# Reordering the recurrence stage of a hybrid encoder block: a planner that follows operands, scores ahead of a bank's first values, merged inverse products

## The chip, the core and the metric

The kernel runs on one core of a Trainium2 chip. The metric is device time in microseconds (us) of one execution. Before the change it is 1988.1 us, the median of three runs (1982.59 to 1990.96). A core has a matrix engine (TensorE, PE in the profile, with PEld its weight loads), a vector engine (DVE), a scalar engine (ACT), GpSimd (POOL), and SyncE (SP), which here issues the DMAs. Each works through its own instructions in order and waits on semaphores for the others. Matrix products land in PSUM, which has eight banks of 128x512 float32.

## The reference, cut to what matters

One encoder layer for a sequence of 1024 positions of width 1024, batch 1:

```
h  = RMSNorm(x);  P = h @ W_in            # latents, RWKV columns, two gates
A  = attention(P)                          # 8 heads, softmax over all 1024 keys
B  = WKV-7 scan forward + WKV-7 scan backward   # 8 heads of 64 x 64 state
     state = state * w_t + (state a_t) b_t^T + v_t k_t^T ;  out_t = state r_t
y  = (sig(gA) * (A @ W_o[:512]) + sig(gB) * (B @ W_o[512:])) @ W_merge
x  = x + y;  x = x + GatedMLP_dwconv3(RMSNorm(x))
```

All arithmetic is float32. The kernel splits large factors into a high and a low part and takes three products for one (the words "hi", "lo", `ph`, `pl`, `wlo` are such parts).

## The kernel before, in words

There are four stages in time. First come the projections and the preparation of all heads' operands. The second stage is the **recurrence stage** that the change is about: it runs on the trace from about 346 us to about 1160 us. Then come the mixture of the branches with `w_merge`, and the feed-forward network.

In the recurrence stage two kinds of work share PE. The **dense** work is a generator, `dense()`: the gate projections (`gates`, line 1153 on, by `mmk`, lines 278 to 281), then `attention` (line 1235 on), then the first branch's output products (`branch0`). The **recurrence** is done in chunks of 64 positions, eight units of 128 positions, both directions at once. For each unit a job `prep_a` makes what the chunks need: decays and keys (`a0` to `a3`), a masked product `NM` (`nm`, `nz`, line 858), which goes through DRAM so that 128 blocks of 16x16 lie one per partition, and the inverse of each block by 15 vector steps (`inv`, tiles `Ti`, `tm`). The inverses go through DRAM again (`dU`, `dT`; step `tq`) and come back as `Un` and `TT` (step `u`, lines 889 to 894: 14 DMAs). Then small products join the blocks to 64x64 inverses: step `p` (line 901), `x` (lines 907 and 914), `y` (lines 925 and 926, into one bank, two products per chunk and half), `t` (line 936). Jobs `prep_b` make the masked products of a chunk (`er`, `ak`, `bt`). The generator `chain` is the recurrence itself: eight hops per unit, each one bank of small products (lines 1019, 1028, 1032, 1046, 1055, 1066) and its eviction. `gnorm` normalizes a unit's output; the last unit's goes on to the mixture.

The order of PE, DVE, ACT and POOL in this stage is that of the program text as it is emitted; only SP's order is the compiler's. A **planner** (line 1423 on) chooses at each turn what to emit, by a clock `now` of its own in estimated ns. `now` moves on by the cost that each generator yields (213 for a product of 512 columns). The wrapper `Clocked` adds up an estimate for DVE, ACT and POOL (`V.t`, `S.t`, `G.t`): it starts an instruction at the later of the engine's last end and `now`. A step of `prep_a` or `prep_b` is due when the steps it needs are seen, when the delay that the step before yielded is over, and when its engine is at most `SLACK` ahead of `now`. A hop of the chain is due when the engines' estimated ends plus `HOP` are past and 1500 ns of dense work (`DENSE`) have gone by since the hop before. If nothing is due, `fill` emits the next piece of dense work. Where the dense work of the last 3400 ns is under 1300 ns, hops and the steps in `HEAVY` wait.

In `attention` a step is one score block (three products, lines 1289 to 1291, in one of three banks `st`), two exponentials or one and a copy, and the low part; four steps later its values are added into the bank `po` (three products, lines 1247 to 1249). After eight of them (one half of the queries of one head) the bank is evicted by a DVE copy `pv` and an ACT logarithm `rc`, and the next half's first values start it anew. There is one `po` bank. The next head's score maxima (`maxima`, line 1217: a product and a DVE reduction) are put beside the steps 3 to 13.

The tile pool `wk` holds one buffer per tag, so a new tile with a tag waits for the readers of the old one. Before, `Un` was one lasting tile of 128x16x32, zeroed once, and the sum `U` of step `x` took the tag `Ti` over from the inverse.

Of the kernel before, what the change touches and what calls it, by code (L numbers as in the profile page):

```python
# [23 lines left out]
NCH = 16  # L24
# [23 lines left out]
LAG = 4  # L48
AHEAD = 6
DENSE = (1500,) * 8  # L50
SLACK = 1500
# [3 lines left out]
CARRY = 3000  # L55
DELAY = {
# [29 lines left out]
def block_kernel(ctx: ExitStack, tc: tile.TileContext, a):  # L86
    nc = tc.nc
    now, ends = [0.0], [0.0]

    class Clocked:  # L90
# [5 lines left out]
        def __getattr__(self, name):  # L96
            f = getattr(self.eng, name)

            def call(*args, **kw):
                o = kw["in_"] if name == "tensor_reduce" else kw["out"] if "out" in kw else args[0] if args else None  # L100
                if hasattr(o, "shape"):
                    self.t = max(self.t, now[0]) + self.fixed + self.each * math.prod(o.shape[1:])
                    ends[0] = max(ends[0], self.t)
                return f(*args, **kw)  # L104
            return call

    V, S, G = Clocked(nc.vector, 140, 1.04), Clocked(nc.scalar, 140, 0.92), Clocked(nc.gpsimd, 100, 2.35)
# [101 lines left out]
    def mm3(ps, wh, wl, xs, first=True, last=True):  # L209
        n = len(xs)  # L210
        for k, (xh, xl) in enumerate(xs):
            ws = slice(k * 128, (k + 1) * 128)
            for hs in halves():
                nc.tensor.matmul(ps[:, hs], wh[:, ws], xh[:, hs], start=(first and k == 0), stop=False)
                nc.tensor.matmul(ps[:, hs], wh[:, ws], xl[:, hs], start=False, stop=False)
            for hs in halves():
                nc.tensor.matmul(ps[:, hs], wl[:, ws], xh[:, hs], start=False, stop=(last and k == n - 1))

    def mm32(ps, w, x, first=True, last=True):
        for hs in halves():  # L220
            nc.tensor.matmul(ps[:, hs], w, x[:, hs], start=first, stop=last)
# [53 lines left out]
    def mmk(outs, wh, wl, x, first, last):  # L275
        xh, xl = x
        for o, hs in zip(outs, HT):
            nc.tensor.matmul(o, wh, xh[:, hs], start=first, stop=False)  # L278
            nc.tensor.matmul(o, wh, xl[:, hs], start=False, stop=False)  # L279
        for o, hs in zip(outs, HT):  # L280
            nc.tensor.matmul(o, wl, xh[:, hs], start=False, stop=last)  # L281
# [5 lines left out]
    with pool("xp") as xp:  # L287
# [61 lines left out]
        for step in XORDER:  # L349
# [10 lines left out]
            else:  # L360
                for hs in HT:
                    ss = ss1()
                    nc.tensor.matmul(ss, onef, acc[:, hs], start=True, stop=True)
# [84 lines left out]
    def gsum(wts, parts):  # L448
        ss = ss1()
        for i, x in enumerate(parts):  # L450
            nc.tensor.matmul(ss, wts, x, start=(i == 0), stop=(i == 1))
# [4 lines left out]
    def mul(ps, w, x, **kw):  # L456
        now[0] += 213 if w.dtype == R else 853
        return nc.tensor.matmul(ps, w, x, **kw)
# [291 lines left out]
    Un = cbp.tile([128, NCH, 32], F32, name="Un")  # L750
    G.memset(Un, 0.0)
# [9 lines left out]
    now[0] = V.t = S.t = G.t = 0.0  # L761
    wpool["g"] = ctx.enter_context(pool("gp", side="right"))
# [43 lines left out]
    def prep_a(n, q):  # L806
# [4 lines left out]
        yield 0, 3000  # L811
# [41 lines left out]
        for c0_ in (0, 8):  # L853
            ps = scb()
            p3 = ps.rearrange("p (c t) -> p c t", t=C)
            for c in range(8):
                for h, hs in enumerate(H):
                    nc.tensor.matmul(p3[hs, c, :], BK[c0_ // 8][hs, c, H[h]], AXk[c0_ // 8][hs, c, :], start=True, stop=True)
# [29 lines left out]
        TT = TTt[n % 2]  # L888
        for g in range(8):
            rows, b = slice(16 * g, 16 * g + 16), g % 4  # L890
            if b != 3:
                nc.sync.dma_start(Un[rows, :, b % 2 * 16:b % 2 * 16 + 16], dU[g].rearrange("c t j -> t c j"))
            nc.sync.dma_start(TT[rows, :, b * 16:b * 16 + 16], dT[g].rearrange("c j t -> j c t"))
        yield 0, 4500
# [5 lines left out]
        for c, r, b in each4:  # L900
            nc.tensor.matmul(p3[r:r + 32, c], NM[r:r + 16, c, b:b + 32], Un[r:r + 16, c, 0:16], start=True, stop=True)
        S.activation(P, p3, AF.Copy, scale=cst[:, C_TI + 1:C_TI + 2])
        yield 1100, 300
        px = scb()[:, 0:256].rearrange("p (c j) -> p c j", j=16)
        for c, r, b in each4:
            if b == 0:
                nc.tensor.matmul(px[r:r + 32, c], TT[r:r + 32, c, 0:32], P[r:r + 32, c], start=True, stop=True)
        U = wk.tile([128, NCH, 16], F32, tag="Ti", name="U")
        for h in range(2):
            ia = slice(h * 64, h * 64 + 32)  # L910
            V.tensor_tensor(out=U[ia], in0=px[ia], in1=Un[ia, :, 0:16], op=add)
        py = scb()[:, 0:256].rearrange("p (c t) -> p c t", t=16)
        for c, r, b in each4:
            nc.tensor.matmul(py[r:r + 16, c], P[r:r + 32, c], TT[r:r + 32, c, b + 16:b + 32], start=True, stop=True)
# [7 lines left out]
        for c in range(NCH):  # L922
            for h in range(2):
                ia, ib = slice(h * 64, h * 64 + 32), slice(h * 64 + 32, h * 64 + 64)
                nc.tensor.matmul(p3[ib, c, 0:16], NM[ia, c, 32:64], U[ia, c], start=True, stop=True)
                nc.tensor.matmul(p3[ib, c, 16:32], NM[ia, c, 32:64], Un[ia, c, 16:32], start=True, stop=True)
# [6 lines left out]
        for c in range(NCH):  # L933
            for h in range(2):
                ia, ib = slice(h * 64, h * 64 + 32), slice(h * 64 + 32, h * 64 + 64)
                nc.tensor.matmul(p3[ia, c], Y[ib, c, :], TT[ib, c, 32:64], start=True, stop=True)
# [6 lines left out]
    def prep_b(n, q, hf):  # L943
# [27 lines left out]
        for c in range(8):  # L971
            for p3, hs in zip(two_, H):
                nc.tensor.matmul(p3[:, c], BK[hs, c, :], AXr[hs, c], start=True, stop=True)
# [8 lines left out]
        for c, d, i in each8:  # L982
            for h, hs in enumerate(H):
                nc.tensor.matmul(p3[H[1 - h], c, :], BK[hs, c, H[1 - h]], AXk[hs, c, :], start=True, stop=True)
# [6 lines left out]
        for d in range(2):  # L991
            ps = scb()
            p3 = ps.rearrange("p (c t) -> p c t", t=128)
            for i in range(4):
                nc.tensor.transpose(p3[:, i, :], BK[:, 4 * d + i, :], ident)
# [11 lines left out]
    def chain(n, q, osb):  # L1007
# [6 lines left out]
        def values(i, RR):  # L1014
            ps = v3(scb())
            vv = q[i][4]
            for s, d, c in EACH:
                for h in range(2):
                    nc.tensor.matmul(ps[H[1 - h], s, :], vv[:, d, c, :], ctr[:, H[h]], start=(s == 0), stop=(s == 7))
# [3 lines left out]
        def chunk_out(i, first, RR):  # L1023
            ct = ctb()
            AXr, Er = q[i][0:2]
            for s, d, c in EACH:
                for h, hs in enumerate(H):
                    nc.tensor.matmul(ct[hs, s, :], RR[h][:, s, 1, :], Er[:, d, c, h, :], start=(s == 0), stop=(first and s == 7))
            if not first:
                for s, d, c in EACH:  # L1030
                    for h, hs in enumerate(H):
                        nc.tensor.matmul(ct[hs, s, :], RR[h][hs, s, 0, :], AXr[hs, s, :], start=False, stop=(s == 7))
# [5 lines left out]
        for i in range(2):  # L1038
# [4 lines left out]
            for s, d, c in EACH:  # L1043
                for h, hs in enumerate(H):
                    ks = H[1 - h] if first else slice(0, 128)
                    nc.tensor.matmul(ct[hs, s, :], Ek[ks, d, c, h, :], RR[h][ks, s, 0, :], start=(s == 0), stop=(s == 7))
# [6 lines left out]
            for s, d, c in EACH:  # L1053
                for hs in H:
                    nc.tensor.matmul(ct[hs, s, :], TT[hs, 8 * i + s, :], rh[hs, s, :], start=(s == 0), stop=(s == 7))
# [8 lines left out]
            for s, d, c in EACH:  # L1064
                for h, hs in enumerate(H):
                    nc.tensor.matmul(ct[hs, s, :], BT[:, d, c, hs], RR[h][:, s, 1, :], start=(s == 0), stop=(s == 7))
# [20 lines left out]
    def gnorm(n, osb):  # L1087
        if n == NU // 2:
            xb.extend([[place(f"h{x}{4 + p}", f"ob{x}") for x in "hl"] for p in range(NPAIR - 1)])
        for d in range(2):  # L1090
# [10 lines left out]
            nc.tensor.matmul(ps, b64r.bitcast(F32), sq, start=True, stop=True)  # L1101
# [12 lines left out]
            for p in range(NPAIR):  # L1114
                cp_ = slice(128 * p, 128 * p + 128)
                nc.tensor.matmul(ps[:, cp_], g2[:, cp_], gl, start=True, stop=True)
# [93 lines left out]
    def maxima(h):  # L1210
# [3 lines left out]
        for qt in range(8):  # L1214
            for i2, hs in enumerate(halves()):
                ps = pt()
                nc.tensor.matmul(ps, qh[0:96, qt * 128:(qt + 1) * 128], kh[0:96, hs], start=True, stop=True)  # L1217
# [6 lines left out]
        nc.tensor.transpose(pm[0:8, 0:128], mx, ident)  # L1224
# [8 lines left out]
    o0, o3 = [], []  # L1233

    def attention():
# [3 lines left out]
        def values(h, q2, kt, ph, pl):  # L1239
# [7 lines left out]
            nc.tensor.matmul(po[0], vhk, ph, start=(kt == 0), stop=False)  # L1247
            nc.tensor.matmul(po[0], vhk, pl, start=False, stop=False)
            nc.tensor.matmul(po[0], vlk, ph, start=False, stop=(kt == 7))
            if kt == 7:  # L1250
# [4 lines left out]
                act(rc[own], po[0][oth], AF.Ln)  # L1255
                if i == 1:
# [16 lines left out]

        def low():
# [3 lines left out]
        for h in range(8):  # L1278
            qh, kh = qk[h % 2]
            nxt = maxima(h + 1) if h < 7 else iter(())  # L1280
            for q2 in range(2):
                qs = HT[q2]
                for kt in range(8):
                    if len(late) == LAG:
# [4 lines left out]
                    nc.tensor.matmul(ps, kh[:, ks], qh[:, qs], start=True, stop=False)  # L1289
                    nc.tensor.matmul(ps, kh[:, ks], ql[:, qs], start=False, stop=False)  # L1290
                    nc.tensor.matmul(ps, kl[:, ks], qh[:, qs], start=False, stop=True)
# [21 lines left out]
                    cost = 640  # L1313
                    late.append((h, q2, kt, ph, pl))
                    step = q2 * 8 + kt
# [4 lines left out]
                    for _ in range(2 if 3 <= step < 11 else 1 if step in (12, 13) else 0):  # L1320
                        cost += next(nxt, 0)
# [104 lines left out]
    B_STEPS = (("b0", 1, None), ("b1", 2, V), ("b2", 1, None), ("er", 1, V), ("ak", 1, V), ("bt", 2, S))  # L1426
# [717 lines left out]
```

## Time and profile before

| what | before |
|---|---|
| median of 3 runs | 1988.1 us |
| the profiled execution's own time | 1986.8 us |
| its span in the trace | 1985.0 us |
| PE busy, whole span | 1859.7 us (94%) |
| DVE, ACT, POOL busy | 1224.6, 870.5, 652.9 us (62%, 44%, 33%) |
| mean granted clock of PE | 0.964 |
| HBM read and written | 144.64 and 59.41 MB |

The profile is of one execution. A row of a group has the line, the engine, the operation, the tiles (out<-in), the shape and the count; then busy time of the group in us, mean ns of one instruction, and the idle time of its engine just ahead of these instructions with what ended it. Where the helper at line 104 records the instruction, all of DVE, ACT and POOL stand under L104 and are told apart by tiles. "issue" is a wait for nothing that the profile shows. A float32 product appears as two records. The granted clock is a share of full speed.

### The profile page before, as it was taken

To read this page: it belongs to the slowest core of one execution; us is meant where nothing else is said; L and a number is where in the kernel's file an instruction comes from. 1 tells how busy PE (TensorE), PEld (TensorE's weight loads), DVE (VectorE), ACT (ScalarE), POOL (GpSimd) and SP (SyncE) were. 2 spreads that over 40 slices of the span, in tenths; PEclk is the share of its full clock that TensorE was granted. 3 is DMA by queue.
4 is the path that set the end of the run, shared out by engine and by line. 5 is a ranking of instruction groups with operands and counts; after the bars stand their busy time and mean duration, and the time that the engine had idled before them with its cause. 6 is when DMAs were issued, how large, how long until landed. Compare 5 with 4: busy or idle time off the path is not lost. (4 is left out here: it accounts for less than half of the span.)

```text
span 1985.0 us, 37748 instructions
## 1 busy us (share of the span) xinstructions
PE 1859.7 (94%) x15440; PEld 1484.7 (75%) x15440; DVE 1224.6 (62%) x1837; ACT 870.5 (44%) x1378; POOL 652.9 (33%) x550
## 2 busy tenths in 40 slices
PE   7889999899999899989989999997999999999998
PEld 5656667677778677777777787775888888888886
DVE  7557666436436466767674345578667667666677
ACT  5576577123223156566666644543233233232331
POOL 7435554322221223343433332235422322322221
PEclk9889999889999898999899999999999999999999
DMA  4136544844454625353432675111111111111112
GB/s 154 36 120 198 176 157 157 227 113 113 121 141 105 176 42 130 80 144 84 112 92 80 215 247 195 41 66 37 49 64 48 48 61 51 48 59 53 48 54 101
DMA packets 260636, 210.71 MB, mean 106 GB/s; under 512 B 127144, under 2 KB 205032, under 8 KB 260464
## 3 DMA queue, kind: packets, MB, share of 16 engines
q1 hardware_dynamic: 260464, 208.31, 35.1%
q8 instruction: 121, 1.98, 0.4%
q14 instruction: 51, 0.42, 0.1%
HBM read 144.64 MB, written 59.41 MB: 103 GB/s over the span
## 5 line engine op out<-in xcount | busy, mean ns | idle before, releaser
L104 POOL TENSOR_TENSOR wlo<-wraw,whi 128x512 fp32r<-128x512 f32 x118 | 161.0, 1365 | 633.0 <-ACT whi L104 613.0
L278 PE MATMUL st<-hh,whi 128*128 128x512 f32 x408 | 175.7, 431 | 22.9 <-ACT hh L104 9.0
L279 PE MATMUL st<-hl,whi 128*128 128x512 f32 x408 | 165.6, 406 | 0.7 <-DVE hl L104 0.7
L104 DVE TENSOR_TENSOR x<-b,x 128x512 f32<-128x512 f32 x176 | 119.2, 686 | 54.6 <-PE b L1817 54.6
L104 POOL TENSOR_TENSOR pl<-pe,ph 128x512 fp32r<-128x512 f32 x64 | 84.3, 1316 | 207.5 <-ACT ph L104 188.8
L281 PE MATMUL st<-hh,wlo 128*128 128x512 f32 x408 | 141.7, 402 | 0.4 <-POOL wlo L104 0.4
L278 PEld LDWEIGHTS st<-hh,whi 128*128 128x128 f32 x408 | 80.1, 196 | 51.5 <-issue 10.8
L104 ACT CAST whi<-wraw 128x512 fp32r<-128x512 f32 x118 | 72.7, 618 | 104.6 <-PE po L279 29.0
L281 PEld LDWEIGHTS st<-hh,wlo 128*128 128x128 f32 x408 | 79.7, 196 | 19.5 <-POOL wlo L104 1.3
L279 PEld LDWEIGHTS st<-hl,whi 128*128 128x128 f32 x408 | 80.3, 197 | 17.6 <-DVE hl L104 1.7
L104 DVE TENSOR_REDUCE mx<-sc 128x1 f32<-128x512 f32 x128 | 81.7, 681 | 12.3 <-PE sc L1217 11.9
L104 POOL TENSOR_TENSOR wl<-wraw,wh 128x512 fp32r<-128x512 f32 x22 | 28.9, 1314 | 179.5 <-ACT wh L104 169.7
L1247 PE MATMUL po<-ph,vhh 128*128 128x512 f32 x128 | 58.9, 460 | 17.6 <-ACT rc L104 17.6
L104 DVE TENSOR_TENSOR u<-b,p 128x512 f32<-128x512 f32 x42 | 29.0, 691 | 72.0 <-PE b L1722 69.4
L1815 PE MATMUL b<-sh,wh 128*128 128x512 f32 x176 | 69.1, 392 | 4.2 <-ACT sh L104 4.2
L1816 PE MATMUL b<-sl,wh 128*128 128x512 f32 x176 | 69.3, 394 | 0.8 <-DVE sl L104 0.8
L1815 PE MATMUL b<-sh,whi 128*128 128x512 f32 x176 | 68.6, 390 | 1.3 <-DVE x L104 1.3
L1817 PE MATMUL b<-sh,wl 128*128 128x512 f32 x176 | 69.0, 392 | 0.0
L1816 PE MATMUL b<-sl,whi 128*128 128x512 f32 x176 | 68.5, 389 | 0.0
L1817 PE MATMUL b<-sh,wlo 128*128 128x512 f32 x176 | 68.5, 389 | 0.0
L104 ACT CAST whi<-s 128x512 fp32r<-128x512 f32 x33 | 20.5, 622 | 89.7 <-PE b L1816 44.0
L1289 PE MATMUL st<-qh,kh 128*128 128x512 f32 x128 | 59.2, 462 | 0.0
(496 smaller groups left out, 5415.4 us busy)
## 6 DMA issues: line engine op xcount, KB each, us to landing
wraw<-w_in SPq DMA_DIRECT2D x64, 256.0 KB
wraw<-w_fd SPq DMA_DIRECT2D x44, 256.0 KB
AA<-w_fu SPq DMA_DIRECT2D x41, 256.0 KB
A<-w_fg SPq DMA_DIRECT2D x41, 256.0 KB
ld<-d_x SPq DMA_DIRECT2D x32, 256.0 KB
d_gate<-gt SPq DMA_DIRECT2D x32, 256.0 KB
xt<-xT SPq DMA_DIRECT2D x8, 512.0 KB
d_s<-sg SPq DMA_DIRECT2D x8, 512.0 KB
```

Of the source, the lines that this page charges most:

```text
L104: return f(*args, **kw)
L278: nc.tensor.matmul(o, wh, xh[:, hs], start=first, stop=False)
L279: nc.tensor.matmul(o, wh, xl[:, hs], start=False, stop=False)
L281: nc.tensor.matmul(o, wl, xh[:, hs], start=False, stop=last)
L1247: nc.tensor.matmul(po[0], vhk, ph, start=(kt == 0), stop=False)
L1289: nc.tensor.matmul(ps, kh[:, ks], qh[:, qs], start=True, stop=False)
L1815: nc.tensor.matmul(b, wh[:, ws], xh[:, hs], start=(k == 0), stop=False)
L1816: nc.tensor.matmul(b, wh[:, ws], xl[:, hs], start=False, stop=False)
L1817: nc.tensor.matmul(b, wl[:, ws], xh[:, hs], start=False, stop=(k == 1))
```

## The change

The diff has these parts; a long run of lines only renames `nc.tensor.matmul` to `E.matmul`, where `E` is a wrapper that issues the same instruction.

- **Estimates that follow operands.** `Clocked` now starts an instruction no earlier than the estimated end of the writers of its operands, by a table `wrote` of tile names. `E` notes in `needs_pe` when the operands of a PE step are there, and `now` is raised to it before the step's cost is added.
- **Constants and rules of the planner.** `SLACK` goes from 1500 to 2500. A new rule (`BATCH`) holds the steps `er`, `ak`, `bt` and `gnorm` back once dense work has begun since the last step or hop, until 2500 of it have gone by. Step `a1` of the first unit is due 18000 after `a0`, not 3000.
- **Attention.** Where the next values are a bank's first (`kt` is 0), the scores and up to two maxima come ahead of them, and the planner may put hops and any steps in between while the estimate says that the bank is not yet evicted by more than 200 (`dense_at`). Maxima stand at steps 3 to 12, not 3 to 13, in the same number.
- **Inverse products.** Step `p` is due 6000 after step `u`, not 4500; step `x` 1500 after `p`, not 300. `Un` becomes a tile of tag `Ti`, zeroed on POOL for each unit; its DMAs are emitted ahead of those of `TT`. `U` and the other part of `Un` now lie side by side in a lasting tile `U2`, and step `y` is one product of 32 columns where two of 16 were.

```diff
-SLACK = 1500
+SLACK = 2500
+BATCH = 2500
...
-                    self.t = max(self.t, now[0]) + self.fixed + self.each * math.prod(o.shape[1:])
+                    out = kw["out"] if "out" in kw else args[0]
+                    names = [x.tensor.name for x in (*args, *kw.values()) if x is not out and hasattr(x, "tensor")]
+                    self.t = max(self.t, now[0], *(wrote.get(x, 0) for x in names)) + self.fixed + self.each * math.prod(o.shape[1:])
                     ends[0] = max(ends[0], self.t)
+                    wrote[out.tensor.name] = self.t
...
+            def call(out, a, b, **kw):
+                needs_pe[0] = max(needs_pe[0], wrote.get(a.tensor.name, 0), wrote.get(b.tensor.name, 0))
+                wrote[out.tensor.name] = 0
+                return f(out, a, b, **kw)
...
-        yield 0, 3000
+        yield 0, 3000 if n else 18000
...
+        Un = wk.tile([128, NCH, 16], F32, tag="Ti", name="Un")
+        G.memset(Un, 0.0)
+        for g in (0, 2, 4, 6, 1, 5):
+            dst = U2[:, :, 16:32] if g % 2 else Un
+            nc.sync.dma_start(dst[16 * g:16 * g + 16], dU[g].rearrange("c t j -> t c j"))
         for g in range(8):
-            rows, b = slice(16 * g, 16 * g + 16), g % 4
-            if b != 3:
-                nc.sync.dma_start(Un[rows, :, b % 2 * 16:b % 2 * 16 + 16], dU[g].rearrange("c t j -> t c j"))
-            nc.sync.dma_start(TT[rows, :, b * 16:b * 16 + 16], dT[g].rearrange("c j t -> j c t"))
-        yield 0, 4500
+            nc.sync.dma_start(TT[16 * g:16 * g + 16, :, g % 4 * 16:g % 4 * 16 + 16], dT[g].rearrange("c j t -> j c t"))
+        yield 0, 6000
...
-        yield 1100, 300
+        yield 1100, 1500
...
-            V.tensor_tensor(out=U[ia], in0=px[ia], in1=Un[ia, :, 0:16], op=add)
+            V.tensor_tensor(out=U2[ia, :, 0:16], in0=px[ia], in1=Un[ia], op=add)
...
-                nc.tensor.matmul(p3[ib, c, 0:16], NM[ia, c, 32:64], U[ia, c], start=True, stop=True)
-                nc.tensor.matmul(p3[ib, c, 16:32], NM[ia, c, 32:64], Un[ia, c, 16:32], start=True, stop=True)
+                E.matmul(p3[ib, c], NM[ia, c, 32:64], U2[ia, c], start=True, stop=True)
...
+        def after():
+            if late and len(late) == LAG:
+                h, q2, kt, ph, pl = late[0]
+                dense_at[0] = max(wrote.get(ph.tensor.name, 0), wrote.get(pl.tensor.name, 0), 0 if kt else po.get("t", 0))
...
-                    if len(late) == LAG:
+                    step = q2 * 8 + kt
+                    if len(late) == LAG and late[0][2]:
                         values(*late.pop(0))
                         yield 640
...
+                    cost = 640
+                    for _ in range(2 if 3 <= step < 11 else 1 if step in (11, 12) else 0):
+                        cost += next(nxt, 0)
+                    if len(late) == LAG:
+                        after()
+                        yield cost
+                        values(*late.pop(0))
+                        cost = 640
...
-                    for _ in range(2 if 3 <= step < 11 else 1 if step in (12, 13) else 0):
-                        cost += next(nxt, 0)
+                    if len(late) == LAG and late[0][2]:
+                        after()
                     yield cost
...
-            now[0] += x[0]
+            now[0] = max(now[0], needs_pe[0]) + x[0]
...
-            if light and (j is norm or j.steps[j.k][0] in HEAVY):
+            if light and (j is norm or j.steps[j.k][0] in HEAVY) or apart and (j is norm or j.steps[j.k][0] in LATER):
                 continue
...
-                if t <= now[0] and due <= 0 and not thin:
+                blocked = dense_at[0] > now[0] + 200
+                if t <= now[0] and (blocked or due <= 0 and not thin):
                     break
-                x = prepare(thin or sparse and t < math.inf)
+                x = prepare(not blocked and (thin or sparse and t < math.inf), not blocked and 0 < alone[0] < BATCH and due > -math.inf)
```

More of the change, by code (lines that the diff above doesn't have):

```diff
@@ L87, in block_kernel @@
     nc = tc.nc
-    now, ends = [0.0], [0.0]
+    now, ends, needs_pe, wrote = [0.0], [0.0], [0.0], {}
     class Clocked:
@@ L277, in mmk @@
         for o, hs in zip(outs, HT):
[L278 to L279 removed]
+            E.matmul(o, wh, xh[:, hs], start=first, stop=False)
+            E.matmul(o, wh, xl[:, hs], start=False, stop=False)
         for o, hs in zip(outs, HT):
[L281 removed]
+            E.matmul(o, wl, xh[:, hs], start=False, stop=last)
     cqps = [big(), big()]
@@ L1027, in chunk_out @@
                 for h, hs in enumerate(H):
-                    nc.tensor.matmul(ct[hs, s, :], RR[h][:, s, 1, :], Er[:, d, c, h, :], start=(s == 0), stop=(first and s == 7))
+                    E.matmul(ct[hs, s, :], RR[h][:, s, 1, :], Er[:, d, c, h, :], start=(s == 0), stop=(first and s == 7))
             if not first:
@@ L1233, in block_kernel @@
     o0, o3 = [], []
+    dense_at = [0.0]
     def attention():
@@ L1488, in run @@
         def run(self):
-            ends[0] = now[0]
+            ends[0], needs_pe[0] = now[0], 0
             x = next(self.gen, None)
@@ L1512, in block_kernel @@
     recent = []
+    alone = [0.0]
     def fill():
         nonlocal due
+        needs_pe[0] = dense_at[0] = 0
         x = next(dn, None)
@@ L1520, in fill @@
         else:
-            now[0] += x * 1.065
+            now[0] = max(now[0], needs_pe[0]) + x * 1.065
             due -= x
+            alone[0] += x
             recent.append((now[0], x))
@@ L1547, in block_kernel @@
                     sparse += 1
+                    alone[0] = 0.0
             if k == 4 and u:
@@ L1551, in block_kernel @@
                 osb = wk.tile([128, 2, 512], F32, tag="osb", name="osb")
-            ends[0] = now[0]
+            ends[0], needs_pe[0] = now[0], 0
             x = next(ch, None)
@@ L1556, in block_kernel @@
             hops = 8 * u + min(k + 1, 7)
-            now[0] += x
+            now[0] = max(now[0], needs_pe[0]) + x
+            alone[0] = 0.0
             ready = max(now[0], ends[0] + x) + HOP
@@ L1721, in quarter @@
             for m, (wt, x) in enumerate(((w[0], xh), (w[0], xl), (w[1], xh))):
-                nc.tensor.matmul(b, wt[:, ws], x, start=(first and k == 0 and m == 0), stop=(k == 3 and m == 2), skip_group_check=True)
+                E.matmul(b, wt[:, ws], x, start=(first and k == 0 and m == 0), stop=(k == 3 and m == 2), skip_group_check=True)
     ps7 = big4()
```

91 lines of the change are left out of this document (49 added, 42 removed).

## The prediction

> **What bounds the kernel now.** I read the page first, then the table of stretches, then PE's waits inside the recurrence stage. The page gives the span, PE at 94%, and PE's own instruction loads (its 30880 records make 1.98 MB, so 64 bytes each).
>
> ```profile
> span 1985.0 us, 37748 instructions
> PE 1859.7 (94%) x15440; PEld 1484.7 (75%) x15440; DVE 1224.6 (62%) x1837; ACT 870.5 (44%) x1378; POOL 652.9 (33%) x550
> ...
> q8 instruction: 121, 1.98, 0.4%
> ```
>
> The stretches (columns: PE, PEld, DVE, ACT, POOL busy, granted clock, DMA share, GB/s) show the stage that changes, and the one after it:
>
> ```profile
> 346.00:1130.00 784.00, 722.37 (x10654) 581.19 (x10652) 434.94 (x860) 350.92 (x628) 235.75 (x253) 0.94 0.47 122
> 1130.00:1200.00 70.00, 70.00 (x315) 57.68 (x314) 35.11 (x45) 33.45 (x45) 23.95 (x23) 1.00 0.74 248
> ```
>
> PE is the bound here: no other engine is busy for much over half. So only three things can be won: PE's idle time (784.0 - 722.4 = 61.6 us), the part of the clock that is not granted (784 x 0.06 = 47 us if PE has work), and PE work that is dropped. The waits of PE in this stage, longest first, say where the idle time is (us in total, times, longest):
>
> ```profile
> PE po L1247 <- ACT rc L104: 17.6, 10, 4.3
> PE sc L914 <- issue: 11.2, 4, 3.8
> PE st L278 <- ACT whi L104: 8.8, 2, 8.6
> PE sc L901 <- DMA Un<-dU: 8.2, 7, 1.9
> PE ct L1046 <- DVE mx L104: 4.9, 3, 2.9
> PE sc L926 <- issue: 3.0, 1, 3.0
> PE sc L907 <- issue: 2.2, 3, 1.0
> ```
>
> These seven rows are 55.9 of the 61.6 us, and every row but the fifth is at a place that the change touches: the first values of a bank, the inverse products, the start of the first unit. The clock goes with them:
>
> ```profile
> 358.80:369.00 10.20, 5.19 (x12) 4.14 (x13) 5.49 (x8) 3.25 (x6) 5.16 (x6) 0.50 0.88 255
> 724.00:727.40 3.40, 1.43 (x6) 0.67 (x4) 2.53 (x5) 1.95 (x4) 0.00 (x0) 1.00 0.11 39
> 727.40:734.20 6.80, 6.80 (x62) 5.76 (x63) 1.36 (x3) 2.14 (x5) 1.27 (x1) 0.50 0.18 41
> 734.20:737.60 3.40, 3.40 (x45) 2.55 (x44) 2.89 (x4) 1.32 (x3) 1.06 (x2) 1.00 0.00 0
> ```
>
> After a stretch of 3.4 us in which PE worked for 1.43 us the clock is at 0.50 for 6.8 us, though PE is busy throughout them, and then full again. A stall of 2 us is thus paid a second time.
>
> **The change part by part.** All is reckoned against the profiled execution (1986.8 us, span 1985.0), which is 1.3 us under the median of the three runs (1988.1); that difference I leave out.
>
> *Merged products.* Step `y` now has two products of 16 columns per chunk and half, and will have one of 32, the shape that step `t` has on the same 32x32 tiles:
>
> ```profile
> L925 PE MATMUL sc<-U,NM 32*32 32x16 f32 x512 | 17.3, 179 | 0.0
> L936 PE MATMUL sc<-TT,Y 32*32 32x32 f32 x512 | 10.0, 195 | 0.0
> ```
>
> The two old products alternate, so the busy time of the one row covers both. The new step costs what `t` costs: 17.3 - 10.0 = 7.3 us saved, all on PE. It also drops 1024 of PE's records (512 products, 512 weight loads), 64 KB of instructions.
>
> *The first unit's `a1` at 18000.* Today DVE reaches the scan of the first unit before its DMA has landed, and ACT and the next weights' high part queue behind it:
>
> ```profile
> 359.73 2.34 DVE L104 TENSOR_TENSOR_SCAN ld<-smask,ld 128x512 f32<-128x512 f32 x2 [8.94 <-DMA ld<-d_s]
> 361.03 0.63 ACT L104 ACTIVATE Pp<-ld 128x512 f32<-128x512 f32 x1 [9.01 <-DVE ld L104]
> 363.81 0.80 PE L278 MATMUL st<-hh,whi 128*128 128x512 f32 x1 [8.56 <-ACT whi L104]
> ```
>
> With 15 us more of dense work ahead of it, the scan stands behind the landing at 359.7 (the stage begins near 346, so its place is near 364). PE's 8.6 us go, and with them the stretch at half clock, 10.2 us, worth 5.1. Ends: 0 (another load is then late) and -13.7; I take -11, near the full price, because the cover of 4 us is real but not large.
>
> *Scores and maxima ahead of a bank's first values.* The bank's eviction waits in DVE's queue:
>
> ```profile
> 724.26 0.39 PE L1291 MATMUL st<-qh,kl 128*128 128x512 f32 x1
> 724.66 0.67 DVE L104 COPY RR<-ct 64x512 f32<-64x512 f32 x1
> 725.26 0.67 DVE L104 COPY pv<-po 64x512 f32<-64x512 f32 x1
> 725.97 0.59 ACT L104 ACTIVATE rc<-po 64x512 f32<-64x512 f32 x1
> 726.62 0.50 PE L1247 MATMUL po<-ph,vhh 128*128 128x512 f32 x1 [1.97 <-ACT rc L104]
> L1217 PE MATMUL sc<-kh,qh 96*128 96x512 f32 x128 | 41.0, 402 | 1.1 <-DMA qh<-d_qrh 1.1
> ```
>
> One more score block (three products that follow each other at about 0.23 us, 0.7 us) and one maximum (41.0/128 = 0.3 us) now stand between: 1.0 us against a mean stall of 1.76, so at most 10 us of 17.6 without more. The planner may add a hop or a preparation step there, so I take -12; ends 0 and -17.6. The held-back exponential of that score block is not needed until four steps later, which hides it.
>
> *Later inverse products, `Un` first.* SP issues the 14 DMAs of step `u` one after another:
>
> ```profile
> L892 SPq DMA_DIRECT2D Un<-dU x48: 302/447/1346, 405.2 to 1068.6; - x48
> L104 POOL MEMSET Un<- x1: 527/527/527, 345.9 to 345.9; 128x512 f32 x1
> ```
>
> The last part that `p` reads was issued twelfth and is now fourth: 8 x 0.447 = 3.6 us earlier, and `p` is 1.5 us later. The longest wait is 1.9, so of 8.2 us I take -7 (if the compiler keeps SP's old order, the 1.5 us alone leave a little). `TT` lands up to 2.2 us later (its first part goes from second to seventh place), but it is read in `x`, which is put off by 1.5 and 1.2 us. The wait that comes in: POOL zeroes `Un` (half of 527 ns, eight times, 2 us) once `Ti` has gone to DRAM; behind it on POOL stand the low parts of weights and exponentials, and PE waits for those. POOL is 33% busy, and step `u` comes 2500 after `tq`; I price it at 0, and at 2 us a unit, 16 us, if that cover is gone.
>
> *The waits on nothing, "issue" (16.4 us).* In the longest of them an instruction load lands (the DMA view of 501.9 to 505.7), in the middle of a run of small products:
>
> ```profile
> 500.76 1.14 PE L914 MATMUL sc<-TT,P 32*16 32x16 f32 x96
> 505.69 0.40 PE L914 MATMUL sc<-TT,P 32*16 32x16 f32 x28 [3.79 <-issue]
> q8 instruction: 1, 0.02, 1.5%
> ```
>
> One load is 1.98 MB/121 = 16 KB, 256 records. By the code steps `p` and `x` have 64 and 96 products, at four records each (two products, two weight loads) 256 and 384 records within a few us, beside a DMA queue full of other things. With 1.2 us more of dense work (few records) between `p` and `x`, and step `y` halved, some of it goes: ends 0 and -16.4, I take -6. The Trainium skill (Runtime: NRT & Kernel Launch, Instruction fetch mechanics) says that crossing a block of instructions costs one DMA tail-bump, "mostly hidden". By it this term would be 0 and the sum 6 us higher; the trace, with 3.79 us of PE idle around such a load, does not agree.
>
> *The clock.* Of the 47 us, 5.1 are counted above; 42 are left. The waits of the last three terms fall by 25 of 42.2 us. A stretch of half clock can outlive a shortened stall, so I take a third of the 42, -14; ends +5 and -42.
>
> *The planner.* Following operands, `SLACK`, `BATCH` and `dense_at` add no instruction. They let DVE run 1000 ns deeper behind PE, and small products share four banks with the maxima: the fifth row of the waits (4.9 us, 3 times, 1.6 each) is such a wait. I reckon six more of them, +10; ends 0 and +25.
>
> Sum: -7.3 - 11 - 12 - 7 - 6 - 14 + 10 = -47.3, so 1986.8 - 47.3 = 1939.5, rounded 1940 us.
>
> **The rivals.**
>
> *The chain falls behind the dense work* (slower). The end of the stage needs both:
>
> ```profile
> L104 POOL TENSOR_TENSOR osb<-gbo,osb x8: 456/462/477, 862.1 to 1152.0; 128x128 fp32r<-128x128 f32 x8
> L281 PE MATMUL po<-o,wlo x16: 388/389/398, 1107.8 to 1158.8; 128*128 128x512 f32 x16
> 613.40:661.60 48.20, 9.02 (x30) 1.00 0.42 119
> ```
>
> The last unit's output is done at 1152.5, the last dense product starts at 1158.8: a margin of 6.3 us. In the order the chain moves back by 15 us at the first unit and by 1.5 + 1.2 = 2.7 us for each of eight units, 36.6 in all. And the inverse of a unit lasts 48.2 us for 9.0 us of DVE (the third row, its `tm` instructions alone): the planner decides its pace. Later estimates of DVE hold it back, the larger `SLACK` lets it go; if the first wins by 5.5 us a unit, 44 more, the lag is 80.6 and the time 1940 + 80.6 - 6.3 = 2014 us. It decides slower from a lag of 6.3 + 47 = 53 us on. For it: the margin is small. Against it: 39 us of each inverse are waiting that the larger `SLACK` can shorten.
>
> *The waits change place* (about the same). The idle times of bank, `Un` and issue come back at other products, the clock stays, and the +10 is paid: 1986.8 - 7.3 - 11 + 10 = 1978.5 us. For it: DVE and ACT still do the same work, and the eviction above waited behind a hop's copy, not behind PE.
>
> *The clock stays as it is*: 1940 + 14 = 1954 us. The half stretches would then come from the small products themselves. The Trainium skill (TensorE: Matmul & The Clock Gate, HAM oscillation — how this bites in real kernels) gives the rule as no idle gaps of PE over about 3.4 us; by it only the longest stalls would count. The row at 724 has a stall of 1.97 us and then 0.50, which speaks against it, so it has a small chance.
>
> *The clock comes back whole*: 1940 - 28 = 1912 us. For it: the stretches of 0.50 above each follow a stall that the change aims at. Against it: the small products stay.
>
> **How the numbers follow.** A measurement of this kernel tells about 0.5% (10 us) from no change, so the bounds are 1978 and 1998 us. Chances: the forecast 0.46, the clock stays 0.12, the clock comes whole 0.10, the waits change place 0.16 (0.04 of it faster, 0.12 the same), the chain behind 0.16 (a lag under 45 us is still faster, 0.02; up to 63 the same, 0.02; beyond it slower, 0.12). Faster: 0.46 + 0.12 + 0.10 + 0.04 + 0.02 = 0.74; the same 0.12 + 0.02 = 0.14; slower 0.12. The range goes from 1912 (half of the whole-clock case below it, 0.05) to 1996 (0.12 above it): 0.17 left out.
>
> **What would show it.** Right: step `y` at about 10 us in all, in half the records; no idle of 8 us near 355; the wait of the values on `rc` under 6 us; the wait for `Un` near 1; mean clock of the stage 0.95 to 0.97; PE's idle time in the stage near 35 us. Wrong: a wait of PE on `mx` or on the low parts above 15 us, stretches of 0.50 as many as before, or PE idle at the end of the stage with `gnorm` as releaser. If the first values still wait 15 us, the eviction is late through DVE's queue, and not for want of PE work.

## The result, and the profile after

The kernel after takes 1939.12 us (median of four runs, 1933.54 to 1941.06); the kernel before, with one more run on the same chip, 1986.78 us. The ratio is 0.9756, with a 95% interval of 0.9726 to 0.9786. The forecast was 1940 us. The page of after gives a span 48.9 us shorter and 1014 instructions fewer (1024 of them are PE's; ten came in elsewhere, eight zeroings on POOL among them); PE's own loads fall from 121 to 117 blocks.

```profile
span 1936.1 us, 36734 instructions
PE 1841.8 (95%) x14928; PEld 1467.8 (76%) x14928; DVE 1229.6 (64%) x1837; ACT 871.1 (45%) x1380; POOL 655.4 (34%) x558
...
q8 instruction: 117, 1.92, 0.4%
```

The table of stretches, first before and then after, from the start of the recurrence stage to the first product with `w_merge`, and from there to the end (length; PE, PEld, DVE, ACT, POOL busy; granted clock, DMA share, GB/s):

```profile
345.40:1202.50 857.10, 795.47 (x10980) 641.44 (x10979) 472.02 (x907) 386.08 (x675) 260.29 (x278) 0.95 0.49 132
1202.50:1985.00 782.50, 755.04 (x3293) 620.59 (x3291) 524.17 (x719) 262.52 (x401) 215.40 (x156) 0.99 0.18 62
```

```profile
345.30:1148.80 803.50, 773.14 (x10469) 623.52 (x10468) 475.09 (x906) 386.57 (x676) 261.48 (x286) 0.97 0.53 140
1148.80:1936.10 787.30, 758.95 (x3293) 622.43 (x3291) 526.94 (x720) 263.56 (x402) 215.83 (x157) 0.98 0.18 62
```

All of the gain is in the stage: 857.1 - 803.5 = 53.6 us; the rest of the kernel, which is the same code, is 4.8 us longer. Of the 53.6 us, PE's idle time gives 31.2 (61.6 to 30.4) and PE's busy time 22.3. PE's waits in the stage of after answer to the seven rows of the prediction (line 123 is the wrapper `E`, line 108 is `Clocked`):

```profile
PE sc L123 <- DMA qh<-d_qrh: 5.7, 3, 4.2
PE sc L123 <- issue: 4.8, 3, 2.4
PE sc L123 <- DVE mx L108: 4.1, 3, 2.2
PE sc L123 <- ACT osb L108: 3.6, 1, 3.6
PE st L123 <- ACT whi L108: 3.1, 1, 3.1
...
PE po L123 <- ACT rc L108: 1.8, 2, 1.6
```

The values' wait on `rc` has gone from 17.6 to 1.8 us and "issue" from 16.4 to 4.8. The wait for `Un` and the 8.6 us at the start of the stage are in no row (the 3.1 us on `whi` come at 1035, where the output products begin). What is new is small and spread out, a head's queries by DMA (5.7) the largest. The groups by line, of after, show the merged step, and that step `p` waits for nothing:

```profile
L123 PE MATMUL sc<-Un,NM 16*32 16x16 f32 x1024 | 10.8, 180 | 0.0
L123 PE MATMUL sc<-U,NM 32*32 32x32 f32 x512 | 9.6, 192 | 0.0
```

17.3 us for 1024 records have become 9.6 for 512. The last output split of a unit and the last dense product, which were 6.8 us apart before, now start in the other order, 1104.5 after 1103.0:

```profile
L108 POOL TENSOR_TENSOR osb<-gbo,osb x8: 454/456/468, 819.2 to 1104.5; 128x128 fp32r<-128x128 f32 x8
L123 PE MATMUL po<-o,wlo x16: 388/389/397, 1046.3 to 1103.0; 128*128 128x512 f32 x16
```

The margin of 6.3 us that the prediction named as the point of its slower rival is used up: the last output now ends 1.5 us after the dense work.

### The profile page after: what moved, and what is told of

It reads as the page before. It is cut to its first block, busy times and chain, and to the rows that moved or that the text cites. A ratio compares the mean times of both kernels' runs of the same rounds, so it can differ in the third digit from the quotient of the medians.

```text
span 1936.1 us, 36734 instructions
## 1 busy us (share of the span) xinstructions
PE 1841.8 (95%) x14928; PEld 1467.8 (76%) x14928; DVE 1229.6 (64%) x1837; ACT 871.1 (45%) x1380; POOL 655.4 (34%) x558
## 5 line engine op out<-in xcount | busy, mean ns | idle before, releaser
L108 ACT CAST whi<-wraw 128x512 fp32r<-128x512 f32 x118 | 72.9, 618 | 110.3 <-issue 30.4
L108 DVE TENSOR_TENSOR pl<-st,ph 128x512 fp32r<-128x512 f32 x64 | 43.6, 683 | 28.3 <-ACT st L108 27.9
```

## Experiments

The theory is that of the prediction: PE bounds the stage, and the parts remove its waits, and with them stretches of half clock. The rival is that the chain and the dense work must end together, and that the planner's order, not the single wait, decides. Twelve kernels were run. The table has ten of them; the two that measure a stall by itself stand further down. "Ratio" is to the kernel before on the same chip, with its 95% interval. "Idle" and "half" are PE's idle time and the time at half clock between the start of the stage and the first product with `w_merge`. "Lag" is the end of the last unit's output less the end of the last dense product of `branch0`. These three are of one execution each. The two kernels that measure a stall have PE's order of after up to `w_merge`, and their half clock there is 38 and 41 us where after has 44, so a few microseconds in that column say nothing.

| kernel | ratio (interval) | idle, us | half, us | lag, us |
|---|---|---|---|---|
| before | 1 | 61.6 | 92 | -7 |
| before, merged `y` | 0.9933 (0.9915 to 0.9951) | 59 | 85 | -7 |
| before, later start | 1.0143 (1.0116 to 1.0170) | 76 | 116 | +49 |
| before, scores ahead | 1.0038 (1.0021 to 1.0055) | 57 | 85 | +1 |
| before, MARGIN 320 | 1.0122 (1.0100 to 1.0145) | 69 | 109 | +6 |
| before, later start, SLACK 2500 | 0.9979 (0.9961 to 0.9996) | 58 | 51 | -7 |
| after | 0.9756 (0.9726 to 0.9786) | 30.4 | 44 | +2 |
| after, MARGIN 320 | 0.9770 (0.9742 to 0.9798) | 35 | 48 | -7 |
| after, SLACK 1500 | 1.0192 (1.0165 to 1.0219) | 86 | 126 | +69 |
| after, blind to operands | 0.9838 (0.9809 to 0.9868) | 40 | 51 | -2 |
| after, old attention order | 0.9967 (0.9947 to 0.9987) | 65 | 75 | +10 |
| after, two more buffers | 0.9736 (0.9715 to 0.9757) | 30 | 31 | +2 |

**The merged step alone.** The order of PE's work stays that of before but for the two products made one.

```diff
-    nc.tensor.matmul(p3[ib, c, 0:16], NM[ia, c, 32:64], U[ia, c], start=True, stop=True)
-    nc.tensor.matmul(p3[ib, c, 16:32], NM[ia, c, 32:64], Un[ia, c, 16:32], start=True, stop=True)
+    nc.tensor.matmul(p3[ib, c], NM[ia, c, 32:64], U2[ia, c], start=True, stop=True)
```

> The kernel before with the merged step y alone (the sum and the second part side by side in a lasting tile of their own, no zeroing per unit; the order of the engines' work is unchanged). Theory of the prediction, that PE work dropped is time gained: 7.3 us less, 1979 to 1980 us against 1987, step y at 10.0 us in all, and the waits on issue somewhat fewer. Rival, that the saved time is spent in the waits next to it (for the inverse's DMAs, for eviction): within 3 us of before.

Measured: 1971.99 us against 1984.8, so 0.67% less, 13 us (10 to 17). In the profiled run of this kernel the span is 15.6 us shorter, 14.3 of it in the stage: 7.5 by the step itself (17.3 to 9.8), 2 of idle time, and the rest by less half clock, which one execution does not secure. The dropped work is a gain in full, and the interval lies above it; what the excess is, the run does not show. The rival falls.

**The later start alone.**

```diff
-        yield 0, 3000
+        yield 0, 3000 if n else 18000
```

> The kernel before with the first unit's a1 due at 18000 instead of 3000, alone. Theory: the idle 8.6 us of PE near 355 and the stretch at half clock behind it go, 11 us less (1976). Rival, re-dealing: the order of all later steps changes too, so the idle time goes but the total lands anywhere within 15 us of before. The idle time near 355 must be gone in both.

Measured: 2014.48 us, 28 us slower. The idle time near 355 is gone, and PE's idle time up to attention falls from 26 to 14 us. But at the end the chain is 49 us behind. The stretches of this kernel, before and after the last dense product:

```profile
1037.70:1134.50 96.80, 89.85 (x1818) 72.79 (x1820) 42.87 (x86) 39.59 (x62) 19.81 (x20) 0.95 0.50 156
1134.50:1181.80 47.30, 27.30 (x394) 22.04 (x394) 12.98 (x26) 17.84 (x36) 12.43 (x18) 0.76 0.26 80
```

In the second stretch there is only the chain left: PE works for 27.3 of 47.3 us, at a clock of 0.76. This is the slower rival of the prediction, brought on by one part of the change alone.

**Scores ahead alone.**

```diff
-                    if len(late) == LAG:
+                    if len(late) == LAG and late[0][2]:
                         values(*late.pop(0))
                         yield 640
...
+                    if len(late) == LAG:
+                        yield cost
+                        values(*late.pop(0))
+                        cost = 640
```

> The kernel before with scores and maxima ahead of a bank's first values alone, without the planner's estimate of the bank's eviction. Theory: the values' wait on rc falls from 17.6 to 6 to 8 us, half clock in the stage falls by some 15 us of stretches, and the time by 10 to 17 us. Rival, the eviction is late through DVE's queue and the wait moves on: the wait on rc falls by less than 5 us, or other waits of PE rise by as much, time within 5 us of before.

Measured: 1991.89 us, 7 us slower; and the wait on `rc` is 1.7 us, down from 17.6. The theory's time is wrong, and of the rival's two signs one came: the eviction is not late through DVE, but other waits rise. PE's waits in the stage of this kernel:

```profile
PE sc L914 <- issue: 13.3, 4, 4.7
PE st L278 <- ACT whi L104: 8.9, 2, 8.5
PE sc L901 <- DMA Un<-dU: 8.7, 8, 1.8
PE sc L1224 <- DVE mx L104: 6.5, 5, 2.4
PE sc L1217 <- DMA qh<-d_qrh: 5.5, 2, 3.7
```

The last two were 2.7 us in all before. In the profiled run the stage is 6 us shorter and the part after it, the same code, 8.6 us longer. So the 16 us won at the bank do not reach the end; where all of them go this run does not settle.

**A control: the same planner, dealt anew.**

```diff
-MARGIN = 300
+MARGIN = 320
```

> Control: the kernel before with the planner's MARGIN at 320 instead of 300, which is for nothing but deals the order of the stage anew. If the terms of the sum are real properties of the parts, the time stays within 4 us of before. If a re-dealt order alone moves the time, it is off by 8 us or more either way, and each one-part experiment is uncertain by that much.

Measured: 2009.22 us, 24 us slower, by an edit that is for nothing (a step is due 20 ns later by the planner's clock). Of the groups of PE's products (runs of one kind) 319 of 6328 stand elsewhere. The wait on `rc` is 29.5 us in 12 times, not 17.6 in 10. So the order of before looks like a good deal, and a part tried alone on it carries a new deal with it: 28 us for the start and 7 for the scores are not clean prices of these parts. Only the merged step, which left the order as it was, is measured cleanly.

**SLACK.** The kernel after with one constant put back:

```diff
-SLACK = 2500
+SLACK = 1500
```

> The kernel after, with SLACK back at 1500, all else as after. Theory that came out of the last runs (chain and dense work must end together, and the larger SLACK pays for the later start by letting the inverses run): the inverses of units 3 to 7 last 30 us or more again instead of 8 to 26, the last unit's output comes after the dense work is out, PE idles and runs at half clock behind it, 1955 to 1985 us. Rival, that SLACK does not matter for the end and only the order is dealt anew: within 10 us of 1939, the inverses as short as after.

Measured: 2020.16 us, a ratio of 1.0192 where after has 0.9756. It is the largest effect of any edit here, outside both expectations, and in the direction of the theory. The inverse's `tm` instructions of the fifth unit, first in after, then with SLACK 1500 (length of the stretch, DVE busy with them; in the kernel before, 35.60 us for 9.25):

```profile
682.00:698.80 16.80, 8.00 (x30) 1.00 0.43 116
```

```profile
749.70:780.10 30.40, 10.06 (x30) 1.00 0.40 107
```

In the second stretch DVE does sixteen maxima between the second instruction of the inverse and the third, in the first none. Over the eight units the inverses last 129 us in after, 181 us with SLACK 1500 and 249 us before. But of the units 4 to 8 only the fifth and the sixth last 30 us or more with SLACK 1500, where the theory had all of them; and the fifth one's inverse begins 68 us later than in after, before it has lost anything itself. So the inverses are a part of the delay. `SLACK` holds back every step of the preparation that has an engine; how much the others lose was not followed up. The chain ends 69 us after the dense work, with PE like this:

```profile
1114.30:1181.50 67.20, 37.54 (x872) 31.94 (x871) 19.92 (x46) 18.79 (x37) 9.79 (x14) 0.68 0.21 58
```

**Later start with the larger SLACK, on the kernel before.**

```diff
-SLACK = 1500
+SLACK = 2500
...
-        yield 0, 3000
+        yield 0, 3000 if n else 18000
```

> The kernel before with the first unit's a1 at 18000 and SLACK at 2500, and nothing else. With the later start alone it took 2014 us, the chain out 29 us after the dense work. Theory, that the larger SLACK pays for the later start: the chain ends ahead of the dense work again, PE's idle time at the end of the stage is under 5 us, and the time is 1965 to 1985 us. Rival, that it takes the new estimates or the other edits too: the chain still ends last, 2000 us or more.

Measured: 1978.55 us, ratio 0.9979. The chain ends 7 us ahead of the dense work again; the last stretch with both has PE busy for 58.69 of 61.10 us:

```profile
1076.70:1137.80 61.10, 58.69 (x502) 47.30 (x502) 20.86 (x34) 33.48 (x48) 21.45 (x22) 1.00 0.67 228
```

From 1.0143 to 0.9979 by one constant: the larger SLACK pays for the later start, as the theory had it. These 33 us are not far above the 24 that a new order alone cost; the end of the chain and the inverses (235 us in all with the later start alone, 179 here) say the same. But the time is only 6 us under before, and the profile flatters this kernel: its execution took 1967.26 us at a mean clock of 0.977, the other nine 1971 to 1983 at 0.965 to 0.974. Idle time in the stage is 58 us: the start's 8.6 are gone, but the chain's products wait 9.4 us for a bank from `mx` where it was 4.9, and step `t` waits 5.1 us for the copies of `Y`.

**Estimates blind to operands.**

```diff
-                    names = [x.tensor.name for x in (*args, *kw.values()) if x is not out and hasattr(x, "tensor")]
+                    names = []
...
-                needs_pe[0] = max(needs_pe[0], wrote.get(a.tensor.name, 0), wrote.get(b.tensor.name, 0))
```

> The kernel after, with the estimates blind to operands as they were before (no table of writers, PE's needs always 0), all other parts kept, dense_at working only from the bank's eviction. Theory A, that true estimates are what keeps PE's waits away: idle time of PE in the stage back from 30 to 45 us or more, 1955 us or later. Theory B, that the structural edits (scores ahead, later products, merged step, first unit later) carry the gain: within 8 us of 1939, the waits on rc, on Un and on issue as low as after.

Measured: 1947.60 us, ratio 0.9838. By the two times it is 8 us later than after; by the two ratios it is 16, because the kernel before took 1982 us on this chip; and it is 11 us later than the next kernel, which has 1936.45 us on the same chip. That lies between the two theories. Idle time is 40 us, with 3.5 on `rc`, nothing for `Un`, 7.5 on "issue" and 8.0 on `mx`, which was 4.1 in after. The edits to the work and the constants carry most of the gain; that the estimates follow operands is worth some 8 to 16 of 48 us here.

**The control on the kernel after.**

```diff
-MARGIN = 300
+MARGIN = 320
```

> Control: the kernel after, with MARGIN at 320 instead of 300. If the new planner's order is less touchy than the old one's (which lost 24 us by the same edit), the time moves by less than 8 us; if a good order is a draw in both, it moves by 8 to 30 us.

Measured: 1936.45 us, ratio 0.9770, no difference from after; 73 of 6322 groups stand elsewhere. The same edit that cost 24 us before costs nothing now. One draw is no proof that the new planner is steadier, but the gain of the change is not one lucky deal.

**The old attention order in the kernel after.** The loop's edits and the hint `dense_at` are undone, all else stays.

```diff
-                    if len(late) == LAG and late[0][2]:
+                    if len(late) == LAG:
                         values(*late.pop(0))
                         yield 640
...
-                    if len(late) == LAG:
-                        after()
-                        yield cost
-                        values(*late.pop(0))
-                        cost = 640
```

> The kernel after, with the attention loop as before: first values ahead of the scores, maxima at steps 3 to 13, no hint of the bank's eviction to the planner. Theory, that this part is worth its wait once the planner is the new one: the values' wait on rc is back at 12 to 20 us and the time is 1948 to 1962 us. Rival, that the wait only moves on (with the old planner this part alone made 7 us more, not less): 1932 to 1945 us, with less of other waits of PE.

Measured: 1977.82 us, ratio 0.9967, some 40 us more than after, well over what the theory gave for the wait alone. The wait on `rc` is back, and others with it:

```profile
PE sc L123 <- DMA qh<-d_qrh: 17.6, 3, 11.5
PE po L123 <- ACT rc L108: 15.5, 9, 4.6
PE b L123 <- ACT obh L108: 6.9, 1, 6.9
```

The chain ends 10 us late, and the first products that read it wait 6.9 us. The inverses last 179 us in all where after has 129, at the same SLACK. A likely cause is that `dense_at` also lets hops and heavy steps through while a bank is evicted, which speeds the chain; this was not tried by itself.

**A stall's price by itself.** In the feed-forward loop of after, ACT copies a bank several times more, and PE's next products wait for it.

```diff
-            S.copy(p1, b)
+            for _ in range(1 + (0, 4, 6, 8, 11)[f % 5]):
+                S.copy(p1, b)
```

> The kernel after, with a stall put into each turn of the feed-forward loop, where PE has hardly any: 0, 4, 6, 8 or 11 more copies of a bank by ACT ahead of the products that write the bank again, so that PE waits 0 to about 5 us, four times each. It measures the price of a stall by itself. Theory, that a stall is paid twice: stalls of 2 us or more are followed by 3.4 to 6.8 us at half clock, most of the time; those under 1 us seldom. By the rule of an idle gap over 3.4 us only the longest stalls, by 11 copies, would be followed by a stretch of half clock.

The second kernel, with other numbers of copies:

```diff
-            S.copy(p1, b)
+            for _ in range(1 + (6, 0, 7, 0, 8, 0)[f % 6]):
+                S.copy(p1, b)
```

> As the kernel with stalls in the feed-forward loop, but with 6, 7 and 8 more copies in every second turn, so that stalls of about 1.7, 2.3 and 2.9 us fall at different times of the clock's windows (in the first one all three stalls of a size fell at the same time of a 3.4 us window). Theory, that a threshold in the stall's length decides: no stretch of half clock after 1.7 us, one of 3.4 us after each of 2.9. Rival, that the place in a fixed window decides: stalls of one size are followed by a stretch in some turns and not in others.

Measured, from the first turn with eight more copies on: the first kernel has stalls of 0.44 us (four), 1.67 us (three), 2.91 to 2.96 us (four) and 4.76 us (four); the second has 1.66, 2.28 and 2.89 us, three of each. The kernels took 1987.54 and 1964.13 us, one run each. Stretches of the second, a stall of 2.28 us and what comes 0.7 us behind it:

```profile
1684.20:1686.50 2.30, 0.04 (x1) 0.04 (x1) 0.06 (x1) 2.21 (x5) 0.00 (x0) 1.00 0.00 0
1687.20:1690.60 3.40, 3.40 (x9) 2.62 (x9) 1.36 (x1) 0.24 (x1) 2.77 (x2) 0.51 0.02 5
1690.60:1694.00 3.40, 3.40 (x16) 2.79 (x16) 0.85 (x2) 1.01 (x2) 0.00 (x0) 1.00 0.59 207
```

At 0.51, 9 products run in 3.4 us, and then 16. Over both kernels, half clock follows none of the four stalls of 0.44 us and none of the six of 1.7, two of three of 2.3, six of seven of 2.9 (3.4 us each) and all four of 4.8 (6.8 us each). The seventh, 2.96 us from 1339.7 on in the first kernel, costs no clock:

```profile
1337.60:1341.00 3.40, 2.13 (x10) 1.44 (x8) 0.78 (x2) 3.21 (x7) 0.00 (x0) 1.00 0.00 0
1341.00:1344.40 3.40, 1.71 (x7) 1.43 (x8) 1.38 (x2) 2.62 (x5) 1.16 (x1) 1.00 0.00 0
1344.40:1347.80 3.40, 3.40 (x16) 2.82 (x15) 2.29 (x2) 0.62 (x1) 3.40 (x3) 1.00 0.13 44
```

So length alone does not decide. In each trace here all changes of the granted clock lie on one grid of 3.41 us. This stall is cut by the grid into 1.26 and 1.70 us. Sorted by the longest part that falls into one step of the grid, the 24 stalls part cleanly: twelve have 2.03 us or more in one step, and the step behind it is at half clock each time; twelve have 1.70 us or less, and none is followed by it. The stalls of 4.76 us have over 2 us in each of two steps, and bring two. The theory of the second kernel, a threshold in length, falls; its rival, the place in time, holds, together with the length.

**Two more buffers.** The kernel after, against its two longest stalls:

```diff
-            t = v3(wk.tile([128, 512], F32, tag="ldb", name="ld2"))
+            t = v3(wk.tile([128, 512], F32, tag="ldb", name="ld2", bufs=2))
...
-                osb = wk.tile([128, 2, 512], F32, tag="osb", name="osb")
+                osb = wk.tile([128, 2, 512], F32, tag="osb", name="osb", bufs=2)
```

> The kernel after with two buffers for the chunk loads of r and v (tag ldb) and two for the units' output (osb), against the two longest stalls that are left: SP held by a load of v that waits for its buffer, so that a head's queries come 4.2 us late, and ACT's copy of the output waiting 7 us for a DMA out of its buffer, which stops PE for 3.6 us. With the half clock behind them (10 and 14 us) theory says 10 to 18 us less than after, 1921 to 1929. Rival, that another wait is next and the order of the DMAs changes: within 5 us of 1938.

Measured: 1930.08 us, ratio 0.9736 (0.9715 to 0.9757). It is the fastest of all kernels here, but its interval overlaps that of after, so its lead over after, 4 us by the ratios, is not secured. ACT's wait at `osb` is gone; the wait for a head's queries is where it was:

```profile
PE sc L123 <- issue: 8.1, 5, 2.7
PE sc L123 <- DMA qh<-d_qrh: 5.7, 3, 4.1
PE st L123 <- ACT whi L108: 4.6, 1, 4.6
```

One stall was read rightly and one wrongly: the buffer of the chunk loads is not what delays the queries.

## Why the prediction was right, and where its steps were not

The time, 1939 against 1940 us, is right, and so is the mechanism in the main: PE's waits at the places named, and the clock behind them. Term by term, by the profiles of before and after:

| term | predicted, us | measured, us | from |
|---|---|---|---|
| merged `y` | -7.3 | -7.7 | 17.3 to 9.6 |
| start of the first unit | -11 | -11.2 | 8.6 idle; half of the 5.19 busy at half clock |
| scores ahead | -12 | -15.8 | 17.6 to 1.8 |
| wait for `Un` | -7 | -8.2 | 8.2 to 0 |
| "issue" | -6 | -11.6 | 16.4 to 4.8 |
| clock, without the start's | -14 | -14.2 | PE busy at half clock 76.9 to 43.3 us, half of it, less 2.6 |
| new waits | +10 | +13 | the other idle time, 10.8 to 23.8 |
| sum | -47.3 | -55.7 | |

The stage gave 53.6, so 2 us are not in these terms, and the part after it took back 4.8, by more half clock in code that did not change. Some of the closeness is luck: the first five terms were 11 us too small together, and the new waits (3 us), the 2 us in no term and the 4.8 us outside the stage took nearly all of it back.

*The clock.* A third of what was left was the right share. But "a stall of 2 us is thus paid a second time" is too simple. Beside full products it is the idle time within one step of the 3.41 us grid that counts, so a stall of 2.28 us was paid twice in two of three cases and one of 2.96 us not at all. Among small products less was enough: in after half clock follows 2.36 us of idle time at 496 but also 0.59 us at 636, both in step `x`; in the two kernels with added stalls, the same place is followed by it after 0.28 and 0.31 us of idle time in the step. The Trainium skill (TensorE: Matmul & The Clock Gate, HAM oscillation — how this bites in real kernels) has no idle gap over about 3.4 us as its rule; here 2.28 us was enough where it lay in one step.

*"issue".* The prediction showed an instruction load beside the longest of these waits. The traces bear this out for all: the nine such waits of over 0.3 us in the stage of before and the three of after each end 1.25 to 1.56 us after the end of a load of PE's instructions.

*"Un first" did not happen.* In after SP issues `TT` for the first unit from 405.5 and `Un` from 411.8, behind the zeroing on POOL (at 409.1, 0.31 us). So it is not the order of the DMAs that took the wait for `Un` away. Nor need it be the later step `p` alone, as the prediction had it for this case: with the later start and the larger SLACK on the kernel before, where `p` comes as early as ever, no wait for `Un` is left either. Which of them did it in after is not shown. The prediction had allowed for SP's order, but thought that then a little would be left.

*The step that failed is the planner's.* The prediction put it down as a cost of +10 us and gave each part a price of its own. The new waits came out at +13. But the runs showed that the parts have no such prices. With SLACK put back, after takes 2020 us: the slower rival of the prediction comes true, the chain 69 us behind the dense work where the rival had 80.6. With the later start alone before takes 2014 us, at a lag of 49 us. With the old attention order after takes 1978 us, 40 us more, where the sum had 12 for this part. The sentence against the rival, that a larger SLACK can shorten the inverse's waiting, pointed at much of it and deserved a term: the inverses went from 249 to 129 us in all. The 16% for the rival was fair for what was known, but SLACK is not its only condition: with the old attention order the chain ends 10 us late at the larger SLACK too.

*Settled and open.* Shown: the merged step's 13 us alone; that the gain goes when the old SLACK or the old attention order is put back; that the larger SLACK brings the chain of the later start back in time; that the operand estimates are worth some 8 to 16 us. Not settled: how the rest divides among scores, hint and later products, since each change of one deals the order anew. Not tried by themselves: `BATCH`, the later steps `p` and `x`, and the larger SLACK on the kernel before.

## What to carry to other kernels

Where an order is made by a planner, run a control that deals it anew before trusting what one part did: here an edit for nothing moved the time by 24 us, more than most parts. Where two streams share an engine, look at which ends first: waits removed from the engine count only as long as the other stream still ends in time, and a constant that speeds that stream can be worth more than any wait. And measure a stall with its clock: on this core stalls under 2 us beside full products cost what they last, and those with over 2 us in one step of the clock's grid half as much again or a little more.

## What the hardware showed that was not expected

- A grid of 3.41 us for the clock: beside full products half clock came after every step of it with 2.03 us or more of idle time in one stall (twelve stalls), and after none with 1.70 us or less (twelve), whatever the length of the stall. It begins with the next step, 2.0 to 4.2 us after the beginning of the stall, so with the longer stalls a part of it falls on idle time.
- Runs of small products stopped in the middle for up to 3.8 us behind a load of PE's instructions: all twelve waits on "issue" in the stage of before and after, eleven of them at small products, ended 1.25 to 1.56 us after such a load.
- The merged step saved 13 us where its own products are 7.5, with the same order of work. Half clock in the stage was 85 us where before had 92, about the difference that one order shows by itself (38 to 44 us), so the excess has no shown cause.
- The part from the first product with `w_merge` on, the same code in all kernels but the two with added stalls, took 781 to 791 us in the profiled runs, with 15 to 28 us at half clock. So the part behind a change can differ by up to 10 us between two profiles though its code does not.
